# A two-layer hybrid trunk on one core: the causal mask moves from TensorE into the keys' row, and two small steps move to GpSimd and to bfloat16

## The chip, the cores and the metric

The kernel runs on one core of one Trainium2 chip: TensorE (PE, matmuls), VectorE (DVE), ScalarE (ACT), GpSimd (POOL) and SyncE (SP, which issues all the DMAs here). The metric is the time of one execution on the device in microseconds, as the median of several runs; lower is better.

## What is computed

Two layers, each a gated mixer over 1024 tokens of width 1024, with 16 heads of 64. Layer 1 is a forgetting attention: a full causal attention whose scores get a decay from a running sum `c` of log-gates. Layer 2 is a windowed attention over three dilations. Cut to what matters here:

```python
def rms_norm(x, g):
    return x * rsqrt(mean(x * x, -1) + EPS) * g

# layer 1, per head, for a block of 128 queries
s = einsum('bqhd,bkhd->bhqk', qi, k) * scale
s = s + ci[..., None] - c_k[:, :, None, :]
s = where(key_pos <= q_pos, s, -inf)
p = softmax(s)
o = einsum('bhqk,bkhd->bqhd', p, v)

# each layer
x = x + (mixer(rms_norm(x, norm_g)) * silu(gate)) @ w_out
```

## The kernel before, in words

**Projections in split float16.** Every float32 matrix is held as a high and a low float16 part. `project` (L693) multiplies 128 tokens by a block of 384 weight columns in 24 matmuls: 8 slices of the width, each as high x high, high x low and low x high. `xh` and `xl` are the two parts of the normed tokens. The weights come as blocks (`Weights`): `load` brings raw float32, `bound` (L630 on ACT, L632 on VectorE, L635) finds a bound of their size per partition in `vm2`, `scale` (L637 on) adds it over the partitions with one matmul against a matrix of ones (`spread_sums`, L602), takes a power of two from it in five small VectorE steps (L604, L592 to L594, L651 or L646), and `split` writes the two float16 parts (L658 on ACT, L659 on VectorE; one quarter by GpSimd, L661 to L663). There are 44 blocks and so 44 such sums.

**Layer 1's attention.** The work goes by pairs of heads (8), and in a pair by tiles of 128 query rows (`fox_tile`, t = 0 to 7). The keys of a tile, (t + 1) x 128 of them, are taken in pieces of 512 columns. For a piece, `scores` (L869) writes q times k into a PSUM bank `s`, two matmuls for each pair of key blocks (256 columns) or single block (128): one with `qk_t` (transposed q and k by DMA), one with `qs` (the same with the parts swapped, copied by VectorE, L849). The piece that holds the diagonal then gets a third matmul, L1114: the identity times a triangle of -1e30 (`ident_b`, `tri_b`, in bfloat16) is accumulated onto the diagonal block. VectorE's reduction (L1116) adds the keys' row `bc` (the running sum `c`, broadcast to 128 partitions by a DMA, L1082, 512 keys each, one for each head and half), negates, and keeps the smallest value. ACT takes the exponent (L912) and the high part (L915), GpSimd subtracts it to get the low part `ph` (L918), a DMA transposes both (L919), and `pv` multiplies by the values (L926 to L928).

**The start.** Eight tiles of x are normed on the way in. The factors of the first two come from columns (`column_factor`: squares on ACT, 8 matmuls with ones, L971, then steps on VectorE and ACT), those of the other six from rows (`row_factor`: squares on ACT, L952; L953, L740 to L742 and the diagonal `dg`, L956, on VectorE; two ACT steps between) and a matmul with ones (L961). `gain_xt` (GpSimd, L986) multiplies by the norm's gain, `split_xt` by the factor and writes `xh` (ACT, L993) and `xl` (VectorE and GpSimd, L994).

**What sets the order.** The program is written with a list of slots (`Flow`), 32 per head pair, one for each two of the 8 slices of a projection. Then `plan_engines` puts every engine's instructions into a fixed order: it takes each with the lengths of a small table (`Step.lasts`), gives it the latest start by which the matmuls, in the order written, would not wait, and lets the engines pick the most urgent that is ready. TensorE starts from the written order. The rotating buffers have counts by tag in `CFG`: `ga` holds the keys' rows and the tiles of x.

## Time and profile before

| | before |
|---|---|
| median of 3 runs | 1662.17 us (1659.58 to 1665.16) |
| profiled execution | 1665.39 us, span 1663.6 us |
| mean granted clock of TensorE | 0.995 |
| moved by DMA | 288.65 MB, mean 174 GB/s |

The span runs from the first to the last instruction of the program; 1.8 us of the profiled execution lie around it. In the rows that follow, a group of instructions reads: line, engine, operation, tile written <- tiles read, shapes, count, then the busy time in us and the mean length of one in ns, then the idle time of the engine ahead of them and who ended it. A row of the timeline has start and length in us. A row of waits has the waiting instruction, the one waited for, the sum in us, the count and the longest. PEld is the load of a matmul's fixed operand, which runs beside other matmuls.

### The profile page before, as it was taken

The numbers are of one execution on the slowest core, as the hardware profiler recorded it, in microseconds if no ns is written. First come the engines' busy times: TensorE is split into PE (matmuls) and PEld (weight loads), VectorE is DVE, ScalarE is ACT, GpSimd is POOL, SyncE is SP. The second block draws the span as 40 slices with busy tenths as digits, with TensorE's granted clock in tenths as the row PEclk, the third lists the DMA queues.
The fourth block names the chain that finished last, engine by engine and source line by source line (L and its number), as shares of the span: only waits on it lengthen the run. The fifth ranks groups of instructions, "written<-read, shape, count | busy, mean of one in ns | idle before, by whom it ended". The sixth has DMA issues, their size and how long they took to land.

```text
span 1663.6 us, 37721 instructions
## 1 busy us (share of the span) xinstructions
PE 1612.1 (97%) x13342; PEld 1045.5 (63%) x13342; DVE 1198.8 (72%) x3695; ACT 1063.0 (64%) x2746; POOL 893.5 (54%) x1049
## 2 busy tenths in 40 slices
PE   5999999999998899999999999999999999999999
PEld 3666677776765447666666666666666666666644
DVE  7857888878876597577676697677776777767751
ACT  6656777777776467566666686666665666666630
POOL 4303666565644242155555566676676766857430
PEclk9999999999999999999999999999999999999999
DMA  7344999999999785247776797668677577768952
GB/s 243 112 134 115 195 214 206 201 188 196 209 202 224 226 252 183 97 110 156 166 156 152 155 227 160 161 160 189 152 168 164 138 191 148 184 159 169 217 163 96
DMA packets 646477, 288.65 MB, mean 174 GB/s; under 512 B 493824, under 2 KB 610560, under 8 KB 646288
## 3 DMA queue, kind: packets, MB, share of 16 engines
q1 hardware_dynamic: 646288, 286.25, 72.7%
q8 instruction: 104, 1.70, 0.4%
q14 instruction: 85, 0.70, 0.2%
HBM read 124.35 MB, written 41.22 MB: 100 GB/s over the span
## 4 chain that ended last, share of the span: by engine, by line
PE 57%; DVE 6%; DMA 4%; issue 2%; ACT 2%; SPq 1%; POOL 1%; DVEq 0%; ACTq 0%; POOLq 0%
PE pj L693 44%; PE pj L718 7%; PE s L869 4%; DMA qk_t<-hl 2%; DVE w L659 1%; PE ob L928 1%; PE ob L926 1%; PE ob L927 1%; DVE xs L1266 1%; DMA ptt<-ph 1%; POOL ph L918 1%; DMA xn_d<-xg 1%; DMA yt<-y_d 1%; ACT w L658 1%; SPq L919 0%
## 5 line engine op out<-in xcount | busy, mean ns | idle before, releaser
L693 PE MATMUL pj<-w,xh 128*128 128x384 f16 (+2 forms) x4864 | 1174.2, 324 | 11.4 <-ACT w L658 4.8
L693 PE MATMUL pj<-w,xl 128*128 128x384 f16 (+2 forms) x2432 | 788.5, 324 | 4.2 <-DVE xl L1271 4.2
L693 PEld LDWEIGHTS <-xh 128*128 128x128 f16 x4864 | 467.3, 98 | 285.1 <-issue 10.6
L693 PEld LDWEIGHTS <-xl 128*128 128x128 f16 x2432 | 238.4, 98 | 160.1 <-issue 6.3
L918 POOL TENSOR_TENSOR ph<-p,ph 128x512 f16<-128x512 f32 (+3 forms) x176 | 174.7, 1012 | 119.5 <-issue 60.0
L1354 POOL TENSOR_TENSOR ph<-p,ph 128x768 f16<-128x768 f32 (+2 forms) x96 | 161.5, 1682 | 138.4 <-ACT ph L1353 131.0
L836 POOL TENSOR_TENSOR hl<-u,hl 128x512 f16<-128x512 f32 x128 | 150.9, 1179 | 71.5 <-ACT hl L835 59.1
L718 PE MATMUL pj<-xh,w 128*128 128x512 f16 x512 | 157.4, 379 | 7.5 <-DVE xr L1232 3.5
L869 PE MATMUL s<-qk_t 128*128 128x128 f16 (+1 forms) x1184 | 151.1, 242 | 4.7 <-DMA qk_t<-hl 4.2
L793 ACT ACTIVATE sq<-pj 128x256 f32<-128x256 f32 x256 | 96.4, 376 | 85.2 <-DVE u L788 84.4
L788 DVE TENSOR_TENSOR u<-pj,gr 128x256 f32<-128x256 f32 x256 | 107.1, 418 | 55.6 <-PE pj L693 54.2
L659 DVE SCALAR_TENSOR_TENSOR w<-raw,sws,w 128x768 f16<-128x768 f32 x96 | 135.4, 1412 | 11.3 <-ACT w L658 11.1
L912 ACT ACTIVATE p<-p,acc 128x512 f32<-128x512 f32 (+2 forms) x192 | 109.4, 607 | 45.0 <-DVE acc L1116 44.8
L718 PEld LDWEIGHTS <-w 128*128 128x128 f16 x768 | 74.0, 98 | 89.1 <-issue 8.9
L1343 ACT ACTIVATE p<-p,og 128x128 f32<-128x128 f32 (+1 forms) x256 | 104.2, 442 | 28.9 <-DVE og L1341 28.0
L926 PEld LDWEIGHTS <-ptt 128*128 128x128 f16 x1136 | 106.1, 98 | 16.5 <-DMA ptt<-ph 5.2
L927 PEld LDWEIGHTS <-ptt 128*128 128x128 f16 x1136 | 105.6, 97 | 11.4 <-issue 0.2
L630 ACT ACTIVATE jk<-raw 128x768 f16<-128x768 f32 (+2 forms) x88 | 72.1, 820 | 55.3 <-DMA raw<-in_w_dsw 36.8
L835 ACT CAST hl<-u 128x512 f16<-128x512 f32 x128 | 78.7, 615 | 45.0 <-DVE u L833 42.3
L1341 DVE CUSTOM_DVE_ANT_0 p<-s,band 128x256 f32<-128x256 f32 (+1 forms) x256 | 90.4, 373 | 23.5 <-PE s L869 23.2
L928 PEld LDWEIGHTS <-ptt 128*128 128x128 f16 x1136 | 105.7, 97 | 0.0
L820 POOL TENSOR_TENSOR ra<-u,cs 128x128 f32<-128x128 f32 x96 | 44.5, 463 | 108.5 <-DVE u L788 98.4
(213 smaller groups left out, 2985.3 us busy)
## 6 DMA issues: line engine op xcount, KB each, us to landing
raw<-in_w_dsw SPq DMA_DIRECT2D x96, 384.0 KB, 4.0
raw<-in_w_fox SPq DMA_DIRECT2D x32, 384.0 KB, 4.2
og_d<-og SPq DMA_DIRECT2D x64, 132.0 KB, 2.4
cmb<-og_d SPq DMA_DIRECT2D x64, 132.0 KB, 2.8
bc<-c_d SPq DMA_DIRECT2D x32, 256.0 KB, 4.0
gs_d<-ge SPq DMA_DIRECT2D x32, 192.0 KB, 2.0
xt<-in_xt SPq DMA_DIRECT2D x16, 256.0 KB, 5.0
gsf<-gs_d SPq DMA_DIRECT2D x64, 64.0 KB, 2.5
```

The costliest lines, as they stand in the source:

```text
L659: nc.vector.scalar_tensor_tensor(w[:, 1, :, :n], raw, self.sw, w[:, 0, :, :n], ALU.mult, ALU.subtract)
L693: nc.tensor.matmul(ps[:, :n], a[:, k, cols], w.slab(k, j), start=(k == 0 and i == 0), stop=(k == KT - 1 and i == 2))
L718: nc.tensor.matmul(ps[m], ws[h].slab(k, j)[:, m * P : (m + 1) * P], a[:, k, 512 * b : 512 * (b + 1)], start=(k == 0 and x == 0), stop=(k = ...
L788: nc.vector.tensor_mul(u[:, t % 2].rearrange("p (a b) d -> p a b d", a=2), ps[:, : 4 * HD].rearrange("p (a b d) -> p a b d", a=2, b=2), gr ...
L836: nc.gpsimd.tensor_sub(hl[:, :, :4, 1], u, hl[:, :, :4, 0])
L869: nc.tensor.matmul(s[:, c0 : c0 + cnt * P].rearrange("p (c s) -> p c s", c=cnt), q, kk[:, j : j + cnt, e], start=(h == 0), stop=(h == 1 an ...
L912: nc.scalar.activation(p, p, AF.Exp, bias=acc, scale=-1.0)
L918: (nc.gpsimd if pool_l else nc.vector).tensor_sub(ph[:, e, 1, cols], p, ph[:, e, 0, cols])
L926: nc.tensor.matmul(o[:, e, :], hi, vt[:, j, e, HD:], start=(b == 0), stop=False, skip_group_check=True)
L927: nc.tensor.matmul(o[:, e, :HD], hi, vt[:, j, e, :HD], start=False, stop=False, skip_group_check=True)
L928: nc.tensor.matmul(o[:, e, :], lo, vt[:, j, e, HD:], start=False, stop=(b == n - 1), skip_group_check=True)
L1354: nc.gpsimd.tensor_sub(ph[:, 1], st["p"], ph[:, 0])
```

## The change

Four things, in one diff. In layer 1's attention the mask matmuls go, with their two constants. The keys' row `bc` becomes 640 wide: 512 keys and ahead of them a slot of 128. For the piece with the diagonal, GpSimd writes into the slot the row's part of the diagonal block plus the triangle (one addition of 128x128 for each head and tile, 128 in all), the scores are written with the diagonal block first, and VectorE's reduction reads the slot and the keys behind it. The probabilities come out in that order, so the value matmuls take the blocks in the order `placed`. The weight bounds are copied into bfloat16 by GpSimd (`vb`) and summed against a bfloat16 matrix of ones. In `row_factor` the five VectorE steps become five GpSimd steps. And the order changes: the first weights' bounds and scale are written ahead of the second tile's factor, the planner starts its engines at 750 and its DMAs at 2400, counts early DMAs 1.35 times, and `ga` gets 8 buffers (7), `qs` 5 (6).

```diff
-    free = dict.fromkeys(ENGINES, 0.0)
+    free = dict.fromkeys(ENGINES, 750.0)
-    pool_end = lock_end = dma_end = 0.0
+    pool_end = lock_end = 0.0
+    dma_end = 2400.0
...
-            dma_end = max(dma_end, t + 500) + x.serves()
+            dma_end = max(dma_end, t + 500) + x.serves() * (1.35 if dma_end < 8000 else 1)
...
-    ident_b = const.tile([P, P], BF16, name="ident_b")
-    nc.vector.tensor_copy(ident_b, ident)
-    tri_b = const.tile([P, P], BF16, name="tri_b")
-    nc.vector.tensor_copy(tri_b, tri)
...
+    ones_b = const.tile([P, P], BF16, name="ones_b")
+    nc.gpsimd.memset(ones_b, 1.0)
...
-        nc.tensor.matmul(ws, ones.bitcast(src.dtype), src, start=True, stop=True)
+        nc.tensor.matmul(ws, by if by is not None else ones.bitcast(src.dtype), src, start=True, stop=True)
...
-            root_scale(f[:, 0:1], spread_sums(self.vm2, KT // 2), 268)
+            vb = sm.tile([P, KT // 2], BF16, name="vb", tag="vb")
+            nc.gpsimd.tensor_copy(vb, self.vm2)
+            root_scale(f[:, 0:1], spread_sums(vb, KT // 2, ones_b), 268)
...
-        nc.scalar.activation(xr, xr, AF.Square, accum_out=v[:, 1:2])
-        nc.vector.tensor_scalar(v[:, 0:1], v[:, 1:2], 1.0 / D, EPS, ALU.mult, ALU.add)
-        inv_sqrt(v[:, 3:4], v[:, 0:1], 1, v[:, 2:3])
+        m, q, a, y = (v[:, i : i + 1] for i in range(4))
+        nc.scalar.activation(xr, xr, AF.Square, accum_out=q)
+        nc.gpsimd.tensor_scalar(m, q, 1.0 / D, EPS, ALU.mult, ALU.add)
+        nc.scalar.activation(y, m, AF.Ln)
+        nc.scalar.activation(y, y, AF.Exp, scale=-0.5)
+        nc.gpsimd.tensor_mul(a, y, y)
+        nc.gpsimd.tensor_mul(a, a, m)
+        nc.gpsimd.tensor_scalar(a, a, -0.5, 1.5, ALU.mult, ALU.add)
         dg = fac[t] = sm.tile([P, P], F32, name="dg", tag="dg", bufs=2)
-        nc.vector.tensor_scalar(dg, ident, v[:, 3:4], None, ALU.mult)
+        nc.gpsimd.tensor_scalar(dg, ident, y, a, ALU.mult, ALU.mult)
...
+    for i in range(KT // 2):
+        w.bound(i)
+    w.scale()
     with book.early(nc, cfg["rush"] / 2):
         nb = column_factor(1)
         gain_xt(1)
         split_xt(1, nb)
-    for i in range(KT // 2):
-        w.bound(i)
-    w.scale()
...
-            bcs[hp, e, h] = lay([P, 512], F32, name="bc", tag="ga")
-            nc.sync.dma_start(bcs[hp, e, h], c_d[2 * hp + e, h * 512 : (h + 1) * 512].partition_broadcast(P))
+            bcs[hp, e, h] = lay([P, 5 * P], F32, name="bc", tag="ga")
+            nc.sync.dma_start(bcs[hp, e, h][:, P:], c_d[2 * hp + e, h * 512 : (h + 1) * 512].partition_broadcast(P))
...
+        a0 = pieces[-1][0] // P
+        placed = [*range(a0), t, *range(a0, t)]
...
-            runs = [(kts[j // 2], j % 2, n) for j, n in key_runs(range(a // P, b // P))]
-            scores(s, kts[t // 2], t % 2, e, runs, b < nk)
+            bc = bcs[hp, e, a // 512]
+            look = key_runs(range(a // P, b // P))
             if b == nk:
-
-                nc.tensor.matmul(s[:, t * P - a : b - a], ident_b, tri_b, start=False, stop=True, skip_group_check=True)
+                look = [[t, 1]] + key_runs(range(a // P, t))
+                nc.gpsimd.tensor_add(bc[:, :P], bc[:, b - a : b - a + P], tri)
+            scores(s, kts[t // 2], t % 2, e, [(kts[j // 2], j % 2, n) for j, n in look])
             acc = st["acc"][:, c : c + 1]
-            nc.vector.tensor_tensor_reduce(p, s[:, : b - a], bcs[hp, e, a // 512][:, : b - a], -1.0, accs[e], ALU.add, ALU.min, acc)
+            nc.vector.tensor_tensor_reduce(p, s[:, : b - a], bc[:, : b - a] if b == nk else bc[:, P:], -1.0, accs[e], ALU.add, ALU.min, acc)
```

**What stands in the engines' orders.** TensorE, in layer 1's attention, the scores of the second query tile (t = 1, two key blocks) for one head of a pair. Before, one pair of blocks and the mask:

```order
L869 LDWEIGHTS qk_t
L869 MATMUL s<-qk_t 128x256
L869 LDWEIGHTS qs
L869 MATMUL s<-qk_t,qs 128x256
L1114 LDWEIGHTS ident_b
L1114 MATMUL s<-tri_b,ident_b 128x128
```

Now the diagonal block and the other block, each alone:

```order
L870 LDWEIGHTS qk_t
L870 MATMUL s<-qk_t 128x128
L870 LDWEIGHTS qs
L870 MATMUL s<-qk_t,qs 128x128
L870 LDWEIGHTS qk_t
L870 MATMUL s<-qk_t 128x128
L870 LDWEIGHTS qs
L870 MATMUL s<-qk_t,qs 128x128
```

The mask's matmul is gone, and where the tile's number is odd two matmuls of 256 columns stand as four of 128.

POOL, in the same stage, from the first tile of a head pair (`ph` of 128x2x128) to the fifth (128x512 and 128x128, the third in time). Before, subtractions and one low part of q and k:

```order
L918 TENSOR_TENSOR ph_4461<-p_4449,ph_4461 128x2x128
L918 TENSOR_TENSOR ph_4535<-p_4523,ph_4535 128x2x256
L836 TENSOR_TENSOR hl_4504<-u_4406,hl_4504 128x8x64
L918 TENSOR_TENSOR ph_4597<-p_4584,ph_4597 128x512
L918 TENSOR_TENSOR ph_4597<-p_4591,ph_4597 128x128
```

Now (`bc_4403` and `bc_4466` are the rows of the second half of the keys for the two heads, `bc_3801` and `bc_4061` those of the first half, `vb` the next weights' bounds):

```order
L919 TENSOR_TENSOR ph_4523<-p_4511,ph_4523 128x2x128
L1122 TENSOR_TENSOR bc_4403<-bc_4403,band_93 128x128
L640 CAST vb_4803<-vm2_4580 128x4
L1122 TENSOR_TENSOR bc_4466<-bc_4466,band_93 128x128
L1122 TENSOR_TENSOR bc_3801<-bc_3801,band_93 128x128
L1122 TENSOR_TENSOR bc_4061<-bc_4061,band_93 128x128
L919 TENSOR_TENSOR ph_4601<-p_4585,ph_4601 128x2x256
L837 TENSOR_TENSOR hl_4566<-u_4468,hl_4566 128x8x64
L1122 TENSOR_TENSOR bc_4403<-bc_4403,band_93 128x128
L1122 TENSOR_TENSOR bc_4466<-bc_4466,band_93 128x128
L919 TENSOR_TENSOR ph_4663<-p_4650,ph_4663 128x512
L919 TENSOR_TENSOR ph_4663<-p_4657,ph_4663 128x128
```

Six additions and the copy have come between the subtractions: the first two of the second half's rows are for the fifth tile, the two of the first half's for the third, the last two for the sixth.

VectorE, in the first 20 us, around the reduction of the first weights' sum (`v<-ws`; `cf` and `nb` are steps of a column factor, `xt` a tile of x). Before:

```order
L975 TENSOR_SCALAR cf<-nb 128x128
L991 TENSOR_TENSOR xt_128<-xt_128,nb 128x512
L604 TENSOR_REDUCE v_240<-ws 128x1
L953 TENSOR_SCALAR nv<-nv 128x1
L632 TENSOR_REDUCE vm<-raw 128x1
L994 TENSOR_TENSOR xl<-xt_126,xh 128x4x128
L592 TENSOR_SCALAR v_240<-v_240 128x1
L632 TENSOR_REDUCE vm<-raw 128x1
L593 TENSOR_SCALAR v_240<-v_240 128x1
L979 SCALAR_TENSOR_TENSOR nb<-nb,cf 128x128
L594 TENSOR_SCALAR ws_f<-v_240 128x1
L980 SCALAR_TENSOR_TENSOR nb<-nb,dg 128x128
```

Now:

```order
L981 TENSOR_SCALAR cf<-nb 128x128
L603 TENSOR_REDUCE v_212<-ws 128x1
L591 TENSOR_SCALAR v_212<-v_212 128x1
L592 TENSOR_SCALAR v_212<-v_212 128x1
L593 TENSOR_SCALAR ws_f<-v_212 128x1
L652 TENSOR_SCALAR ws_f<-ws_f,sx 128x1
L985 SCALAR_TENSOR_TENSOR nb<-nb,cf 128x128
L653 RECIPROCAL ws_f<-ws_f 128x1
L986 SCALAR_TENSOR_TENSOR nb<-nb,dg 128x128
L997 TENSOR_TENSOR xt_124<-xt_124,nb 128x512
L631 TENSOR_REDUCE vm<-raw 128x1
L997 TENSOR_TENSOR xt_126<-xt_126,nb 128x512
```

The weights' chain, spread between other steps before and behind the first tile, stands in one piece ahead of the first tile's multiply.

More of the change, by code (lines that the diff above doesn't have):

```diff
@@ L594, in root_scale, with spread_sums @@
         nc.vector.tensor_single_scalar(dst.bitcast(I32), e, 0x7F800000, ALU.bitwise_and)
-    def spread_sums(src, n):
+    def spread_sums(src, n, by=None):
         if under.get("ps") is not None:
@@ L862, in key_runs, with scores @@
         return runs
-    def scores(s, qk, i, e, keys, more):
+    def scores(s, qk, i, e, keys):
         c0 = 0
@@ L873, in scores @@
                     start=(h == 0),
-                    stop=(h == 1 and not more),
+                    stop=(h == 1),
                     skip_group_check=True,
@@ L1128, in score @@
                 for i in range(2):
-                    ptl[i] = [(pt[:, i, 0, j], pt[:, i, 1, j], j) for j in range(t + 1)]
+                    ptl[i] = [(pt[:, i, 0, k], pt[:, i, 1, k], j) for k, j in enumerate(placed)]
             else:
@@ L1133, in score @@
                 pt = p_transpose(1, nk, exps, splits)
-                ptl[e] = [(pt[:, 0, 0, j], pt[:, 0, 1, j], j) for j in range(t + 1)]
+                ptl[e] = [(pt[:, 0, 0, k], pt[:, 0, 1, k], j) for k, j in enumerate(placed)]
         def values(e):
@@ L1332, in score @@
                 for e in range(2):
-                    scores(ss[i][:, 2 * e * P :], qks[1], i, e, keys, False)
+                    scores(ss[i][:, 2 * e * P :], qks[1], i, e, keys)
             for i in range(2):
@@ L1500, in trunk @@
     layer["cm"].__exit__(None, None, None)
-CFG = dict(out={(False, 0): (), (True, 0): ((18, 20, 22, 24), (0, 0, 1, 1), 3, (4, 6, 8, 10)), (True, 1): ((18, 20, 22, 24), (14, 15, 17, 18), 24, (33, 35, 37, 39))}, take=(((33, 34, 37, 40), 42), ((62, 63, 66, 69), 71)), rush=2000, gate=(((6, 7, 8, 9), (0, 0, 1, 1), 4, (5, 6, 7, 9)), ((44, 45, 46, 47), (26, 28, 30, 32), 36, (38, 40, 42, 44)), ()), bc=((1, 0, 26), (1, 1, 28), (0, 0, 38), (0, 1, 46)), wpool=3, rbufs=8, most=(0, 2), lcm=7, ps=0, pv=100, ph_=100, ph=1, wbufs=8, pl=3, um=3, lpf=8, lsd=((16, 16), (16, 14), (14, 11)), ty2=((0, 4), (1, 5)), hb=2, ub=2, qb=1, nb=3, fox=(((0, 0, 2, 2), (2, 4)), ((0, 0), (4, 4))), due=(29, 33, 39, 45, 35, 41, 49, 57), l1=dict(ga=7, ptt=4, ph=3, p=4, qk_t=6, qs=6, vt=3, gsl=3), l2=dict(ga=4, cmb=4, gsd=4, ptt=3, ph=3, p=2, qk_t=3, og=3, vt=3, gsl=3, par=1), wload=(18, 20, 22, 24), wbound=(0, 1, 3, 4), wscale=8, wsplit=(10, 16, 22, 12))
+CFG = dict(out={(False, 0): (), (True, 0): ((18, 20, 22, 24), (0, 0, 1, 1), 3, (4, 6, 8, 10)), (True, 1): ((18, 20, 22, 24), (14, 15, 17, 18), 24, (33, 35, 37, 39))}, take=(((33, 34, 37, 40), 42), ((62, 63, 66, 69), 71)), rush=2000, gate=(((6, 7, 8, 9), (0, 0, 1, 1), 4, (5, 6, 7, 9)), ((44, 45, 46, 47), (26, 28, 30, 32), 36, (38, 40, 42, 44)), ()), bc=((1, 0, 26), (1, 1, 28), (0, 0, 38), (0, 1, 46)), wpool=3, rbufs=8, most=(0, 2), lcm=7, ps=0, pv=100, ph_=100, ph=1, wbufs=8, pl=3, um=3, lpf=8, lsd=((16, 16), (16, 14), (14, 11)), ty2=((0, 4), (1, 5)), hb=2, ub=2, qb=1, nb=3, fox=(((0, 0, 2, 2), (2, 4)), ((0, 0), (4, 4))), due=(29, 33, 39, 45, 35, 41, 49, 57), l1=dict(ga=8, ptt=4, ph=3, p=4, qk_t=6, qs=5, vt=3, gsl=3), l2=dict(ga=4, cmb=4, gsd=4, ptt=3, ph=3, p=2, qk_t=3, og=3, vt=3, gsl=3, par=1), wload=(18, 20, 22, 24), wbound=(0, 1, 3, 4), wscale=8, wsplit=(10, 16, 22, 12))
 def host_layout(inputs):
```

## The prediction

> **What bounds the kernel now.** I read the page first, for the shares of the engines:
>
> ```profile
> span 1663.6 us, 37721 instructions
> PE 1612.1 (97%) x13342; PEld 1045.5 (63%) x13342; DVE 1198.8 (72%) x3695; ACT 1063.0 (64%) x2746; POOL 893.5 (54%) x1049
> ```
>
> TensorE is busy for 97% of the span; it leaves 51.5 us over. A share of the whole span says nothing on a stage, so the second view is the busy time by stage: the stretch up to 60 us is the start, 130 to 450 most of the eight head pairs of layer 1's attention, 450 to 560 its tail. The columns are PE, weight loads, DVE, ACT and POOL busy, then the granted clock, the DMA share and GB/s.
>
> ```profile
> 0.00:20.00 20.00, 6.86 (x36) 6.50 (x37) 9.75 (x35) 11.51 (x27) 7.41 (x15) 1.00 0.82 289
> 20.00:40.00 20.00, 16.42 (x90) 9.57 (x90) 19.16 (x39) 14.19 (x30) 11.67 (x11) 0.83 0.58 189
> 130.00:300.00 170.00, 169.11 (x1711) 118.46 (x1709) 138.22 (x439) 124.00 (x317) 97.32 (x93) 1.00 0.86 187
> 300.00:450.00 150.00, 148.05 (x1579) 105.78 (x1577) 125.07 (x406) 112.62 (x282) 93.20 (x91) 1.00 0.95 201
> 450.00:560.00 110.00, 98.21 (x946) 63.89 (x945) 71.58 (x210) 73.97 (x157) 52.89 (x50) 0.98 0.94 210
> ```
>
> In the attention TensorE is idle for 2.8 of 320 us, while DVE is 82% and POOL 60% busy: matmuls set the time there, and a matmul that is taken out is time won as long as nobody else becomes late. In the first 40 us TensorE is idle for 16.7 us: there the chain that feeds it sets the time. The third view, TensorE's waits in 130 to 450 us, holds only two lines:
>
> ```profile
> PE s L869 <- DVE qs L849: 1.3, 2, 0.7
> PE o L926 <- DMA ptt<-ph: 1.2, 1, 1.2
> ```
>
> The same view up to 60 us names the start's (us in total, times, longest):
>
> ```profile
> PE pj L693 <- ACT w L658: 4.8, 1, 4.8
> PE pj L693 <- DVE w L659: 4.2, 3, 1.8
> PE nb L961 <- DVE nv L953: 0.6, 1, 0.6
> ```
>
> **The mask matmuls.** The groups by form give their count, and the timeline of TensorE at one of them its price in the stream (start, length):
>
> ```profile
> L1114 PE MATMUL s<-tri_b,ident_b 128*128 128x128 bf16 x128 | 27.7, 220 | 0.0
> ```
> ```profile
> 252.74 0.27 PE L869 MATMUL s<-qk_t,qs 128*128 128x256 f16 x1
> 252.85 0.22 PE L869 MATMUL s<-qk_t 128*128 128x128 f16 x1
> 252.91 0.22 PE L869 MATMUL s<-qk_t,qs 128*128 128x128 f16 x1
> 252.96 0.22 PE L1114 MATMUL s<-tri_b,ident_b 128*128 128x128 bf16 x1
> 253.02 0.27 PE L869 MATMUL s<-qk_t 128*128 128x256 f16 x1
> ```
>
> The 220 ns of a matmul overlap with its neighbours; what it costs is the distance to the next start: 0.055 us for 128 columns (252.91, 252.96, 253.02), 0.11 for 256. 128 masks x 0.056 = 7.2 us leave the stream. Against that, the diagonal block now stands alone and first, so a row tile with an odd number loses its last pair of key blocks: 8 head pairs x 4 odd tiles x 2 heads = 64 times, two matmuls of 256 columns become four of 128, 4 x 0.056 - 2 x 0.109 = 0.006 us, together 0.4 us. Net 6.8 us.
>
> **What GpSimd gets for it.** 128 additions of 128x128. The trace has the same shape, two operands from SBUF, in another stage, and beside it the work that POOL has in the attention (130 to 530 us):
>
> ```profile
> L820 POOL TENSOR_TENSOR ra<-u,cs x96: 446/453/1266, 704.3 to 1566.2; 128x128 f32<-128x128 f32 x96
> ```
> ```profile
> L918 POOL TENSOR_TENSOR ph<-p,ph 128x512 f16<-128x512 f32 x102 | 119.0, 1176 | 110.8 <-issue 56.2 <-ACT ph L915 25.7 <-ACT rs_y L827 15.8
> ```
>
> 128 x 0.45 = 58 us over about 370 us of attention take POOL from 60% to some 76%: off the path as long as each addition ends before VectorE wants the row. In the order, the additions for a tile stand four to ten POOL instructions ahead of its own subtraction, and VectorE wants the row some three ahead of that; an instruction there takes about 1 us, so I cost the place at nothing. What is queued behind an addition that waits for its row's DMA is the subtraction of another tile, and its transpose and value matmuls behind that; the issue to landing of a row is 4.0 us at the median, and a row is asked for at least 7 of a head pair's 32 slots ahead of its first use, 7 x 47 / 32 = 10 us. The second cost lies on VectorE, whose operations slow down when POOL works:
>
> ```profile
> L849 DVE TENSOR_SCALAR qs<-qk_t x64: 286/346/1274, 140.0 to 511.9; 64x256 int32<-64x256 int32 x64
> L659 DVE SCALAR_TENSOR_TENSOR w<-raw,sws,w x96: 999/1182/2894, 97.3 to 1512.4; 128x768 f16<-128x768 f32 x96
> ```
>
> The lowest and the largest length differ by one long POOL operation. The Trainium skill states the rule behind that ("SBUF — State Buffer", section "SBUF: two separate sides"): VectorE and GpSimd share a pair of ports, an instruction holds it to its end, and an instruction of the other that needs it waits. It speaks against this change, since every addition is one more holder; the trace agrees as far as the spread of these two rows goes. From the rows alone: some 11 such VectorE operations per head pair (8 qs, 3 weight splits) could each be held for up to 0.45 us, 5 us of the 8 us that VectorE has idle in a head pair (18% of 47 us). At POOL's added share (16%) it is nearer to 1 us. I take +1.2 us for the whole stage (bounds 0 and 7, the latter the whole gain).
>
> **The sums of the weight bounds.** 44 matmuls of 128x4 go from float32 to bfloat16. Two that follow each other, and the stream around the second:
>
> ```profile
> 300.86 0.30 PE L602 MATMUL pj<-vm,ones 128*128 128x4 f32 x1
> ...
> 336.21 0.19 ACT L635 ACTIVATE vm<-vm 128x2 fp32r<-128x2 f32 x1
> ...
> 347.12 0.49 PE L693 MATMUL pj<-w,xh 128*128 128x384 f16 x2
> 347.45 0.33 PE L693 MATMUL pj<-w,xl 128*128 128x384 f16 x1
> 347.48 0.30 PE L602 MATMUL pj<-vm,ones 128*128 128x4 f32 x1
> 347.64 0.50 PE L693 MATMUL pj<-w,xh 128*128 128x384 f16 x2
> 347.98 0.33 PE L693 MATMUL pj<-w,xl 128*128 128x384 f16 x1
> ```
>
> From 347.45 to 347.98 stand three projection matmuls, 3 x 0.163 = 0.49 us of 0.53: the sum costs 0.04 us. (From 300.86 to 347.48 is a head pair, 47 us, the figure used above.) A bfloat16 one can save between nothing and all of it, 0 to 1.8 us over 44; I take 0.3. The copy into bfloat16 lies on POOL between the bound and the sum. This bound had its last piece at 336.4, 11 us ahead of the matmul, which covers it; where a new layer's weights follow at once that cover is gone, and two or three times up to 0.5 us show: +0.3.
>
> **The start.** The rows that carry it:
>
> ```profile
> 10.03 0.83 ACT L630 ACTIVATE jk<-raw 128x768 f16<-128x768 f32 x1
> 10.97 1.26 ACT L969 ACTIVATE xsq<-xt 128x512 f32<-128x512 f32 x2
> 14.55 1.04 ACT L952 ACTIVATE xrow<-xrow 128x1024 f32<-128x1024 f32 x1
> 15.17 0.25 PE L602 MATMUL ws<-vm,ones 128*128 128x4 f32 x1
> 16.79 0.16 DVE L604 TENSOR_REDUCE v<-ws 128x1 f32<-128x4 f32 x1
> 19.28 3.41 ACT L658 ACTIVATE w<-raw,ws_f 128x768 f16<-128x768 f32 x4
> 20.26 0.32 PE L693 MATMUL pj<-w,xh 128*128 128x384 f16 x1 [4.84 <-ACT w L658]
> 25.36 0.52 PE L693 MATMUL pj<-w,xl 128*128 128x384 f16 x1
> 26.15 1.00 DVE L659 SCALAR_TENSOR_TENSOR w<-raw,ws_f,w 128x768 f16<-128x768 f32 x1
> ```
>
> Today the first weights' bounds are ready at about 11, but the sum stands on TensorE behind the second tile's column sums (15.17), its reduction on VectorE behind that tile's work (16.79), and the first half of the weights is written from 19.28. The change puts the sum ahead of the second tile. Then: copy on POOL until 11.3, sum and five small VectorE steps until 12.5. ACT is next in the way: its order holds two steps of the first factor (0.6), the row's squares (1.2), the third step (0.3) and the second tile's squares (1.26) ahead of the split, 10.9 + 3.4 = 14.3. First weights at 15.2, xh of the first tile at 15.9: TensorE starts at about 16 in place of 20.26. VectorE writes the four low halves in between other steps, the last at about 22.6 in place of 27.15 (it waits for ACT's third step of tile 1 at about 21). So the first tile's 24 matmuls are done near 24. The second tile needs its factor behind that, then a multiply of 0.7 and a cast of 0.6: about 25.5. Before, 9 of the 24 had started by 25.4. Ahead by 15 x 0.163 = 2.4 us. Behind it comes the factor of the third tile, now on POOL behind a step that waits for ACT; and 1.8 us of waiting for the second weight block (the longest of the three above) that may fall away, since VectorE is rid of five small steps per tile. I take 3.0 us for the start, bounds 0 (all of it waits again for the third tile's factor) and 5.4 (2.4 + 1.8 + two waits of 0.6).
>
> **The sum.** -7.2 + 0.4 - 0.3 + 1.2 + 0.3 - 3.0 = -8.6 us. The profiled execution took 1665.39 us (1.8 around its span) and lies 3.2 above the median of 1662.17; taken off the median the forecast is 1653.6. The rest of layer 1's tail and layer 2 stand in the same order as before, so nothing is booked there.
>
> **The rivals.** *The attention gives it back.* The 6.8 us return as waits of TensorE on qs, on transposes or on DMA (its share is 0.95 in 300 to 450, and in the tail, 450 to 560, TensorE is idle for 11.8 us). Against it: 2.5 us of waits in 320, and none on the rows. Then only the start is won: 1662.2 - 3.0 = 1659.2, no measurable change. *Slower: the additions come late.* If they wait on POOL behind subtractions that wait themselves, VectorE stands before its reduction with everything behind it. VectorE has 8 us idle in a head pair and 16 additions: up to 0.5 us each is free, and there it decides. Ten of 16 late by one subtraction (1.18 us) would be 11.8 - 8 = 3.8 us per head pair, 30 in all: 1684. For it speak POOL's waits before the subtractions (the row of L918: 110.8 us idle), against it that the additions stand ahead of their tile by several of these. *Full clock from the start.* TensorE waited 4.8 us in one piece ahead of 20.26, and from there the clock fell to 0.83 over 20 us, 3.4 us lost. After the change, by the working above, no piece reaches 3 us. If the clock then never falls, up to 3.4 us more: 1650.2. The Trainium skill has this as a rule ("TensorE: Matmul & The Clock Gate", section "What's actually happening"): an idle window of about 3.4 us brings half clock, and as long a busy one ends it. The trace agrees in that the fall follows its longest wait; that the wait shrinks is only my estimate. *The start wins nothing*, as a wait on the third tile's factor takes its place: 1662.2 - 5.6 = 1656.6.
>
> **How the numbers follow.** Three runs of before lie 5.6 us apart; 0.3% (5.0 us) is about what can be told from no change, so faster means below 1657.2. Forecast 0.52, of it 0.48 below that line; given back 0.20, all within; full clock 0.10, faster; start without gain 0.10, half of it on each side; late additions 0.08, slower. Faster 0.63, same 0.29, slower 0.08. The range goes down to the full clock with the start's upper bound (1650.2 - 2.4, less another 0.8 for the sums' own bound) 1647, and up over the case of a given-back gain by what a median can be off, to 1662; outside lie the late additions and a little more.
>
> **What would show it.** Right: no line for the mask, 256-column score matmuls fewer by 128 and 128-column ones more by 256; 128 additions of about 0.45 us; in 130 to 450 us still under 5 us of TensorE waits; first projection matmul near 16; an attention shorter by 6 us. Wrong: VectorE's reductions waiting on the additions, qs longer by a third with TensorE behind it, or the first 60 us without more matmuls than before.

## The result and the profile after

| | before | after |
|---|---|---|
| median of 6 runs | 1662.30 us (1659.58 to 1665.16) | 1652.52 us (1652.01 to 1656.83) |
| ratio to before | | 0.9936 [0.9922, 0.9949] |
| profiled execution | 1665.39 us, span 1663.6 | 1656.83 us, span 1654.8 |

The kernel is faster by 9.8 us at the median. The profiled executions differ by 8.6 us, the same as the sum of the forecast; each is the slowest of its six. In the tables below, places in the stream are marked by the start of a projection matmul that both programs have: the 701st (in the first head pair, 137.84 us before) ends the start, the 2113th (600.87 us) is the first of layer 2.

| in the profiled execution | before | after | difference |
|---|---|---|---|
| first projection matmul | 20.26 | 16.38 | -3.9 |
| end of the start (701st) | 137.84 | 133.43 | -4.4 |
| from there to layer 2 (2113th) | 463.03 | 458.44 | -4.6 |
| layer 2 and its end | | | +0.2 |

First the stages of after, with the same columns as before: PE, weight loads, DVE, ACT and POOL busy, then the granted clock, the DMA share and GB/s.

```profile
0.00:20.00 20.00, 11.39 (x49) 8.95 (x50) 11.66 (x32) 14.02 (x30) 10.18 (x20) 1.00 0.92 335
20.00:40.00 20.00, 16.29 (x92) 9.56 (x91) 17.82 (x31) 15.10 (x37) 19.46 (x29) 0.91 0.53 185
130.00:300.00 170.00, 165.86 (x1716) 115.98 (x1714) 135.29 (x443) 124.62 (x316) 126.27 (x158) 1.00 0.92 192
300.00:450.00 150.00, 148.96 (x1638) 106.75 (x1637) 125.31 (x411) 116.68 (x290) 118.85 (x147) 1.00 1.01 206
```

In the first 40 us TensorE is busy for 4.4 us more (27.7 against 23.3). In 130 to 450 POOL went from 60% to 77%, and TensorE's idle time from 2.8 to 5.2 us. Its waits in that stretch name where (5.1 us in all; the forecast had set under 5 as a sign of being right):

```profile
PE o L927 <- DMA ptt<-ph: 4.1, 4, 1.5
PE s L870 <- DVE acc L1125: 1.0, 1, 1.0
```

The waits for `qs` are gone; those for transposed probabilities went from 1.2 to 4.1 us. The additions, by form, with the idle time of GpSimd ahead of them and who ended it:

```profile
L1122 POOL TENSOR_TENSOR bc<-bc,band 128x128 f32<-128x128 f32 x128 | 65.6, 524 | 28.3 <-DMA bc<-c_d 13.3 <-DVE acc L1125 13.1 <-ACT w L659 1.1
```

An addition is 0.52 us at the mean (0.46 at the median), but GpSimd also stands still for 28.3 us in front of them: 13.3 for the row's DMA, 13.1 for the reduction that still reads the slot for the tile before. From 130 to 450 us it is 15.2 us. One such wait can be followed to TensorE. On GpSimd's timeline the second row waits, with two subtractions behind it; on SP's the row was asked for at 216.92, and the transpose of the first of those subtractions, issued at 218.56, is held for 5.56 us; on TensorE's the value matmul then waits:

```profile
218.40 1.23 POOL L1122 TENSOR_TENSOR bc<-bc,band 128x128 f32<-128x128 f32 x1
221.88 0.45 POOL L1122 TENSOR_TENSOR bc<-bc,band 128x128 f32<-128x128 f32 x1 [2.25 <-DMA bc<-c_d]
222.30 2.08 POOL L919 TENSOR_TENSOR ph<-p,ph 128x512 f16<-128x512 f32 x2
```
```profile
216.92 0.57 SPq L1088 DMA_DIRECT2D bc<-c_d  x1
218.56 5.56 SPq L920 DMA_TRANSPOSE ptt<-ph  x1
```
```profile
226.15 0.20 PE L927 MATMUL o<-vt,ptt 128*128 128x65 f16 x1 [1.47 <-DMA ptt<-ph]
```

This row is asked for 5 us ahead of its first reader, not 10: the planner put the addition far ahead of VectorE's use. In 8 of the 32 rows the addition waits for the DMA like this. So there were two theories for what the attention gives back: waits at the head of GpSimd's queue (A), or DMAs that are full and bring transposes late whoever adds (B).

The start, on the timeline:

```profile
10.20 0.19 POOL L640 CAST vb<-vm 128x4 bf16<-128x4 f32 x1 [0.20 <-ACT jk L629]
10.43 0.16 PE L601 MATMUL ws<-vb,ones_b 128*128 128x4 bf16 x1 [0.46 <-POOL vb L640]
13.17 0.92 ACT L659 ACTIVATE w<-raw,ws_f 128x768 f16<-128x768 f32 x1
16.38 0.85 PE L694 MATMUL pj<-w,xh 128*128 128x384 f16 x2
20.58 1.01 DVE L660 SCALAR_TENSOR_TENSOR w<-raw,ws_f,w 128x768 f16<-128x768 f32 x1
23.73 0.50 PE L694 MATMUL pj<-w,xh 128*128 128x384 f16 x2
```

The walk of the forecast holds within a microsecond or two: copy at 10.2 (forecast until 11.3), weights from 13.2, first matmul at 16.38 (16), last low half done at 21.6 (22.6), second tile from 23.7 (25.5).

### The profile page after: what moved, and what is told of

The parts are those of the page before. It is cut to its first block, busy times and chain, and to the rows that moved or that the text cites. A ratio compares the mean times of both kernels' runs of the same rounds, so it can differ in the third digit from the quotient of the medians.

```text
span 1654.8 us, 37873 instructions
## 1 busy us (share of the span) xinstructions
PE 1605.9 (97%) x13342; PEld 1037.5 (63%) x13342; DVE 1192.6 (72%) x3663; ACT 1063.5 (64%) x2746; POOL 963.9 (58%) x1252
## 4 chain that ended last, share of the span: by engine, by line
PE 74%; DVE 10%; DMA 6%; ACT 4%; issue 3%; POOL 2%; SPq 0%; DVEq 0%; POOLq 0%; ACTq 0%
PE pj L694 56%; PE pj L719 7%; PE s L870 6%; DMA qk_t<-hl 3%; DVE w L660 2%; DVE p L1125 1%; PE ob L929 1%; PE ob L927 1%; PE ob L928 1%; DMA ptt<-ph 1%; ACT w L659 1%; PE o L929 1%; PE o L927 1%; PE o L928 1%; DVE xl L1280 1%
## 5 line engine op out<-in xcount | busy, mean ns | idle before, releaser
L1363 POOL TENSOR_TENSOR ph<-p,ph 128x768 f16<-128x768 f32 (+2 forms) x96 | 157.7, 1642 | 137.6 <-ACT ph L1362 130.1
L660 DVE SCALAR_TENSOR_TENSOR w<-raw,sws,w 128x768 f16<-128x768 f32 x96 | 146.6, 1528 | 11.0 <-ACT w L659 10.7
L1350 DVE CUSTOM_DVE_ANT_0 p<-s,band 128x256 f32<-128x256 f32 (+1 forms) x256 | 90.7, 373 | 22.8 <-PE s L870 22.6
```

The lines of the kernel that those rows point to most:

```text
L660: nc.vector.scalar_tensor_tensor(w[:, 1, :, :n], raw, self.sw, w[:, 0, :, :n], ALU.mult, ALU.subtract)
L1363: nc.gpsimd.tensor_sub(ph[:, 1], st["p"], ph[:, 0])
```

## The experiments

All ratios are to the kernel before, run on the same chip. 0.001 is 1.7 us. The kernel before stood in every set of runs, the changed kernel in the first set alone, so a difference between two runs is one of ratios. The three columns at the right are differences to before in the profiled execution, in us; one execution differs from another of the same kernel by several us, so they tell where, and the ratios how much.

| run | ratio [interval] | start | attention and its tail | layer 2 |
|---|---|---|---|---|
| changed kernel | 0.9936 [0.9922, 0.9949] | -4.4 | -4.6 | +0.2 |
| e1, zero matmuls added | 1.0000 [0.9989, 1.0012] | -4.9 | +3.1 | +0.9 |
| e2, masks by matmul | 0.9973 [0.9962, 0.9984] | -4.8 | -2.9 | -0.3 |
| e10, new mask alone | 0.9995 [0.998, 1.0009] | -0.5 | +0.4 | +4.3 |
| e3, a quarter of the additions | 0.9947 [0.9928, 0.9966] | -4.3 | -4.6 | +3.5 |
| e4, each addition twice | 1.0047 [1.0033, 1.0061] | -4.4 | +13.9 | +1.3 |
| e11, rows early | 1.0039 [1.0024, 1.0054] | -4.0 | +9.4 | +0.8 |
| e12, new mask alone, rows early | 1.0061 [1.0037, 1.0086] | +0.7 | +6.0 | +0.9 |
| e13, additions planned later | 1.0022 [1.0009, 1.0035] | -4.2 | +6.3 | -0.5 |
| e14, additions on VectorE | 1.0010 [0.9998, 1.0022] | -4.0 | +1.9 | +2.5 |
| e8, sums in float32 | 0.9956 [0.994, 0.9972] | -6.8 | -0.8 | +2.4 |
| e5, first scale late | 0.9954 [0.9938, 0.9971] | -4.0 | -3.7 | +1.4 |
| e6, row factors on VectorE | 0.9970 [0.9955, 0.9985] | -1.5 | -5.9 | +5.5 |

**e1: is a mask matmul worth 0.056 us?** The changed kernel with 128 matmuls of the old size put back, on zeros. (The scores of the diagonal block, the only thing that they write, do not survive them: the result lacks these, and the kernel stands for its time alone.)

```diff
...
-            scores(s, kts[t // 2], t % 2, e, [...])
+            scores(s, kts[t // 2], t % 2, e, [...], b == nk)
+            if b == nk:
+                nc.tensor.matmul(s[:, :P], ones_b, zero_b, start=False, stop=True, skip_group_check=True)
```

> The changed kernel, with 128 matmuls of 128x128 bfloat16 put back where the mask's stood; they add zeros, so the additions on GpSimd still do the masking. Theory of the stream (a matmul taken out of the attention is time won): 128 x 0.056 = 7.2 us come back, 1659.5 to 1660. Rival, that the attention was gained by the order and the buffers and not by the matmuls: within 1.5 us of the changed kernel, 1651 to 1654. Between the two: part of the stream's time lay in waits anyway.

The whole gain goes: 0.0064 +- 0.0018 or 10.6 us over the changed kernel, and 7.7 us in the stage itself (+3.1 against -4.6). The price of 7.2 is near the stage's figure and just under the lower end of the other (7.6 to 13.6 us).

**e2: everything but the mask.** The changed kernel with the old mask scheme (two constants, `bc` 512 wide, blocks in their old order).

```diff
-                look = [[t, 1]] + key_runs(range(a // P, t))
-                nc.gpsimd.tensor_add(bc[:, :P], bc[:, b - a : b - a + P], tri)
...
+                nc.tensor.matmul(s[:, t * P - a : b - a], ident_b, tri_b, start=False, stop=True, skip_group_check=True)
```

> The changed kernel with the mask as before (matmul of the identity and the triangle, keys' row of 512 without a slot, key blocks in their old order), everything else changed. Theory of the stream: 6.8 us come back less the 1 us or so that the additions cost, 1657 to 1659. Theory that the additions cost nothing: 1659. Rival, order and buffers: 1652 to 1654.

The rest alone gives 4.5 us at the median. So in this company the mask is worth 0.0037 +- 0.0017, or 6.2 us, where the forecast had 5.6 (7.2 - 0.4 - 1.2). The profiled executions show less of it: the start of e2 has -4.8, but its attention -2.9 too, which leaves 1.7 for the mask. (That execution of e2 is the second fastest of its twelve, the changed kernel's the slowest of its six.) What the mask took out of the stream shows in TensorE's busy time between the 701st and the 2113th projection matmul, before, in e2 and after:

```profile
137.84:600.87 463.03, 448.40 (x4370) 302.03 (x4368) 362.17 (x1105) 330.75 (x778) 255.43 (x239) 1.00 0.92 207
133.08:593.22 460.14, 448.56 (x4371) 300.90 (x4368) 356.87 (x1106) 332.51 (x779) 258.79 (x250) 1.00 0.93 208
133.43:591.87 458.44, 441.86 (x4370) 295.32 (x4369) 359.01 (x1106) 330.81 (x779) 314.50 (x376) 1.00 0.96 209
```

With the mask by matmul TensorE is busy for 448.4 and 448.6 us, without it for 441.9: 6.5 and 6.7 us less, where the forecast had 6.8. (The clock stood at half for 3.4 us of the stage in each of the three.) Its idle time is 14.6, 11.6 and 16.6 us. From 130 to 450 us e2 idles for 2.9 us, as before; so the 2.3 us more in the changed kernel come with the new scheme.

**e10: the mask without the rest.** The kernel before with the slot, the additions, the new order of blocks and the buffer counts.

```diff
-CFG = dict(... l1=dict(ga=7, ..., qs=6, ...) ...)
+CFG = dict(... l1=dict(ga=8, ..., qs=5, ...) ...)
...
+                look = [[t, 1]] + key_runs(range(a // P, t))
+                nc.gpsimd.tensor_add(bc[:, :P], bc[:, b - a : b - a + P], tri)
```

> The kernel before with the new mask alone (slot, additions, key order, and the buffer counts 8 and 5), start and sums as before. Theory of the stream: 1662.3 - 5.5 = 1657, with the attention shorter by 4 to 6 us and the first 130 us as before. Rival, that the start carries nearly all: 1661 to 1662.

No measurable gain, 0.8 us; the rival of this run came out. The same edit is worth 6.2 us in one company and 0.8 in another. In its profile the matmuls did leave the stream: between the same two projection matmuls TensorE is busy for 445.6 us (448.4 before), although the clock stood at half for 10.2 us of the stage there (3.4 before), and it idles for 17.8 us (14.6 before). That execution is 5.8 us slower than the median of its kernel. Why the gain is lost in this company isn't settled: the other edits also move the order that the planner gives, and e11 and e13 below show what another order of the same work can do.

**e3: fewer additions.** Only the tiles t = 0 and 4 get an addition (32 of 128; the other tiles read the slot as that one left it, with the triangle but with another block's part of the row).

```diff
+                if t % 4 == 0:
                     nc.gpsimd.tensor_add(bc[:, :P], bc[:, b - a : b - a + P], tri)
```

> The changed kernel with the addition written only for the first tile of each keys' row, 32 in place of 128; the other tiles read the slot as that one left it, so their mask and keys' term in the diagonal block are left wrong. If the additions lie beside other work: within 1.5 us, 1651 to 1654. If they hold up VectorE or the subtractions (the shared ports, the queue), three quarters of what they cost goes: 1647 to 1650, with fewer waits of value matmuls on transposes.

As the changed kernel (0.0011 +- 0.0023 above it). 42 us less of GpSimd's work from 130 to 450 us buys nothing that shows, so between 32 and 128 the number is no cost that can be told. What remains is the first addition on each row, which waits for its DMA (6.6 us in 8 waits): that spoke for theory A. But TensorE's waits for transposed probabilities were to fall with the additions and didn't: 7.0 us in seven, 4.1 in the changed kernel.

**e11: the rows earlier.** One line, and the same work.

```diff
-CFG = dict(... bc=((1, 0, 26), (1, 1, 28), (0, 0, 38), (0, 1, 46)), ...)
+CFG = dict(... bc=((1, 0, 16), (1, 1, 18), (0, 0, 28), (0, 1, 36)), ...)
```

> The changed kernel with one line other: the keys' rows are asked for 10 slots of 32 (some 15 us) earlier. Theory A (rows too late for their new first reader): in the changed kernel an addition that waits for its row's DMA stands at the head of GpSimd's queue and holds subtractions, transposes and value matmuls behind it (6.1 us in 5 waits from 130 to 450 us, and 4.9 us of TensorE waits for transposed probabilities over the run). With the rows early the additions' waits for a DMA fall below 2 us, TensorE's waits for transposes fall by 2 to 4 us, and the time is 1649 to 1651 where the changed kernel has 1652.5 (ratio to before 0.992). Rival B (the transposes are late because the DMAs are full, share 0.92 to 1.0): the additions stop waiting but TensorE waits for transposes as before, 4 to 6 us; ratio 0.9935, no change to the changed kernel. Rival C (order): the rows now come in between transposes that are urgent, and the time rises by 1 to 4 us.

The sign is rival C's, the size none of the three: slower than the changed kernel by 0.0103, 17 us. TensorE's waits from 130 to 450 us, then those of GpSimd's additions:

```profile
PE o L927 <- DMA ptt<-ph: 6.5, 7, 1.8
PE s L870 <- DVE acc L1125: 2.4, 3, 1.0
PE pj L694 <- DVE u L834: 2.1, 1, 2.1
PE s L870 <- DMA qk_t<-hl: 1.6, 2, 0.9
```
```profile
POOL bc L1122 <- DVE acc L1125: 13.4, 13, 2.7
POOL bc L1122 <- DMA bc<-c_d: 7.0, 6, 2.2
```

An addition that is ready earlier in the plan is also put earlier in GpSimd's order. It waits no less for the row (7.0 against 6.1 us), and longer for the reduction that still reads the slot (13.4 against 7.4); with the smaller ones the waits grew from 15.2 to 28.0 us.

**e12: the mask alone, rows early.** The same line in e10.

> The kernel before with the new mask alone (slot, additions, buffer counts 8 and 5) and the keys' rows asked for 10 slots earlier. With the rows at their old slots this part alone gave a ratio of 0.9995. Theory A (late rows ate the mask's gain): the gain of 6.8 us shows up, at least 4 of it: ratio 0.996 to 0.9975. Rival B (DMA saturation or another order ate it): 0.999 to 1.001 again. Rival C (the gain is lost behind the attention, in layer 2, by another order of the planner): the attention ends 3 to 6 us earlier in the trace than before and the total does not.

11 us slower than e10. Asking earlier does not bring the mask's gain back. It is no clean test of late rows, though: the additions moved forward with the rows, and from 130 to 450 us they wait for them longer than in e10 (17.8 us against 9.7).

**e4: each addition twice.**

```diff
                 nc.gpsimd.tensor_add(bc[:, :P], bc[:, b - a : b - a + P], tri)
+                nc.gpsimd.tensor_add(bc[:, :P], bc[:, b - a : b - a + P], tri)
```

> The changed kernel with each of the 128 additions issued twice (the second writes the same values again): 58 us more of GpSimd's work over 370 us, its share in the attention from 77% to about 92%. With a quarter of the additions (32) the ratio was 0.9947, with 128 it is 0.9936: no price for their number so far. Theory A (the number costs nothing while GpSimd has room, only waits at the head of its queue cost): within 3 us of the changed kernel, ratio 0.993 to 0.9955. Rival B (shared port: each addition costs VectorE or TensorE a little): +1.2 us for 128 as the forecast had it, ratio 0.9945. Rival C (GpSimd becomes the bound of the attention, subtractions late at every tile): +5 to +30 us, ratio 0.997 to 1.012.

Rival C: +18 us over the changed kernel, at 85% busy of GpSimd in 130 to 450 us against 77%. That GpSimd has no room left at 85% is the plain reading, but not shown: the order is another one too, and e13 below loses 14 us at 74%.

**e13: the additions later.** In the planner, an addition counts as ready 1 us later.

```diff
-                ready[j] = max(ready[j], end[k] + tail + SIGNAL[q] + margin[q])
+                ready[j] = max(ready[j], end[k] + tail + SIGNAL[q] + margin[q] + (1000 if q == "Pool" and steps[j].outs[0].name.startswith("bc") else 0))
```

> The changed kernel with the planner told that an addition can start 1 us later behind what it waits for, so that on GpSimd it is put later, behind subtractions; the work is the same. Asking for the rows 10 slots earlier moved the additions forward in GpSimd's order: their waits at the queue's head went from 15 to 28 us between 130 and 450 us, and the time up by 17 us. Theory A (waits at the head of GpSimd's queue): the additions' waits fall below 10 us, and the time is 1648 to 1653 (ratio 0.991 to 0.994). Rival B (any other order than the one found for these lengths is worse, since the order was fitted to them): ratio 0.997 to 1.005 with the waits for the additions no longer than in the changed kernel. Rival C: the additions now come too late for VectorE's reductions, which then wait on them in the trace: over 5 us of such waits, ratio above 0.998.

Slower than the changed kernel by 14 us, though the additions' waits fell from 15.2 to 11.6 us in 130 to 450 (theory A had asked for under 10):

```profile
PE o L927 <- DMA ptt<-ph: 5.8, 4, 2.4
PE s L870 <- DVE acc L1125: 3.4, 3, 1.7
PE pj L694 <- DVE u L834: 1.4, 1, 1.4
```
```profile
POOL bc L1122 <- DVE acc L1125: 10.5, 8, 2.5
POOL bc L1122 <- DMA bc<-c_d: 1.1, 1, 1.1
```

TensorE's waits went up to 10.6 us all the same. So theory A falls as the one cause: the length of the waits at the head of GpSimd's queue doesn't order the results (11.6 us in e13, 15.2 after, 28.0 in e11). Rival B of this run, another order is a worse one, is what came out; what in the order does it stays open.

**e14: nothing of it on GpSimd.**

```diff
-                nc.gpsimd.tensor_add(bc[:, :P], bc[:, b - a : b - a + P], tri)
+                nc.vector.tensor_add(bc[:, :P], bc[:, b - a : b - a + P], tri)
```

> The changed kernel with the 128 additions on VectorE, whose reductions stand behind one another anyway; GpSimd has none. Theory A (what eats the mask's gain is GpSimd's queue: an addition that waits at its head for a row or for the reduction that reads its slot, 15 us in 5 + 12 + 1 + 1 waits from 130 to 450 us, holds subtractions, transposes and value matmuls): TensorE's waits for transposed probabilities fall from 4.1 us to under 2 in that stretch, and the time is 1649 to 1652 (ratio to before 0.991 to 0.993), as long as VectorE, 81% busy there, has room for 128 x 0.25 us = 32 us more (10%). Rival B (transposes are late because the DMAs are full, whoever adds): the waits for transposes stay, ratio 0.9936 as the changed kernel. Rival C (VectorE becomes late): waits of TensorE on VectorE's qs and reductions, 5 to 15 us, ratio 0.997 to 1.003.

Rival C. TensorE's waits, and the two stages:

```profile
PE s L870 <- DVE qs L850: 6.3, 4, 2.0
PE o L927 <- DMA ptt<-ph: 2.9, 5, 1.1
```
```profile
130.00:300.00 170.00, 164.18 (x1693) 114.13 (x1692) 155.22 (x485) 122.39 (x310) 96.65 (x96) 1.00 0.91 186
300.00:450.00 150.00, 145.51 (x1591) 103.31 (x1590) 142.56 (x460) 114.64 (x285) 93.37 (x94) 1.00 0.98 206
```

VectorE goes from 81% to 93%, and its `qs` comes late for 6.3 us. The waits for transposes fall only from 4.1 to 2.9 with no addition in GpSimd's queue at all. They don't follow the additions in the other profiles either: 1.2 before and 2.6 in e2, both without additions, 7.0 in e3 with a quarter of them.

**e8: the sums in float32**, without the copy `vb`.

```diff
-            vb = sm.tile([P, KT // 2], BF16, name="vb", tag="vb")
-            nc.gpsimd.tensor_copy(vb, self.vm2)
-            root_scale(f[:, 0:1], spread_sums(vb, KT // 2, ones_b), 268)
+            root_scale(f[:, 0:1], spread_sums(self.vm2, KT // 2), 268)
```

> The changed kernel with the 44 sums of the weight bounds in float32 again, without the copies to bfloat16 on GpSimd. The forecast had -0.3 us for the bfloat16 matmuls (bounds 0 to -1.8) and +0.3 for exposed copies: together nothing, ratio 0.9936 and the first projection matmul within 0.3 us of 16.4. Rival: a float32 matmul of 4 columns stops the stream for more than the 0.04 us read from one place (weight load of 128x128 float32 in four passes); then 44 x 0.1 to 0.3 us come back, 4 to 13 us, ratio 0.996 to 1.001.

0.0020 +- 0.0021 above the changed kernel, no difference that can be told. (Its profile has a start shorter by 2.4 us and an attention longer by 3.8; one profile can't tell whether these are the edit's.) The rival's weight load took 0.19 us in float32 before (at 347.45) where bfloat16's takes 0.10 (at 296.60), beside running matmuls. In the stream of the changed kernel one sum stands like this:

```profile
296.60 0.33 PE L694 MATMUL pj<-w,xl 128*128 128x384 f16 x1
296.76 0.17 PE L601 MATMUL pj<-vb,ones_b 128*128 128x4 bf16 x1
296.79 0.48 PE L694 MATMUL pj<-w,xh 128*128 128x384 f16 x2
297.12 0.32 PE L694 MATMUL pj<-w,xl 128*128 128x384 f16 x1
```

Three projection matmuls and the sum take 0.52 us where before they took 0.53: 0.01 x 44 = 0.4 us saved, an estimate at the resolution of the rows.

**e5 and e6: which edit made the start.** e5 writes the first weights' bounds and scale behind the second tile's factor again; e6 gives the row factors' five steps back to VectorE.

```diff
-    for i in range(KT // 2):
-        w.bound(i)
-    w.scale()
     with book.early(nc, cfg["rush"] / 2):
...
+    for i in range(KT // 2):
+        w.bound(i)
+    w.scale()
```
```diff
-        nc.gpsimd.tensor_scalar(m, q, 1.0 / D, EPS, ALU.mult, ALU.add)
...
+        nc.vector.tensor_scalar(v[:, 0:1], v[:, 1:2], 1.0 / D, EPS, ALU.mult, ALU.add)
+        inv_sqrt(v[:, 3:4], v[:, 0:1], 1, v[:, 2:3])
...
+        nc.vector.tensor_scalar(dg, ident, v[:, 3:4], None, ALU.mult)
```

> The changed kernel with the bounds and the scale of the first weights written again behind the second tile's factor. The start (to the 700th projection matmul, ahead of the attention) ends 4.4 us earlier in the changed kernel than in the one before; the forecast had 3.0, all from this move. If so: first projection matmul at 19 to 20.5 where the changed kernel has 16.4, and the start's gain falls to 0 to 1.5 us; ratio 0.995 to 0.997. Rival (the row factors on GpSimd and the planner's constants bring it): the first matmul goes back but the start keeps over 2.5 us of its gain.

> The changed kernel with the five small steps of the row factors on VectorE again. The forecast had up to 1.8 us for VectorE's relief in its bound, not in its value, and 0 as the other end if the third tile's factor is late on GpSimd. Theory A: the start's gain falls from 4.4 to 2.6 to 4 us; ratio 0.994 to 0.995. Rival (GpSimd's factors come later than VectorE's would, three waits of 0.3 to 0.8 us on the factor's diagonal in the changed kernel): the start gains 0.5 to 1.5 us more, ratio 0.9925 to 0.9935.

| start of a projection matmul | before | changed | e5 | e6 |
|---|---|---|---|---|
| 1st | 20.26 | 16.38 | 19.95 | 17.35 |
| 24th (last of the first tile) | 29.09 | 22.30 | 28.35 | 27.91 |
| 701st | 137.84 | 133.43 | 133.82 | 136.36 |

Without the early scale the first matmul comes late again, and the start still wins 4.0 us. With it and without the moved factors the first matmul comes early and 1.5 us are left. (The seven other runs that keep the moved factors, the early scale and the copy have -4.0 to -4.9; e8, without the copy, -6.8.) TensorE's waits up to 60 us in e5, then in e6:

```profile
PE nb L967 <- POOL dg L962: 1.2, 2, 0.8
PE pj L694 <- DVE w L660: 0.8, 1, 0.8
```
```profile
PE pj L694 <- DVE w L660: 5.6, 4, 2.8
PE nb L962 <- DVE nv L954: 0.7, 1, 0.7
```

In e6 TensorE waits for the weights' low halves on VectorE, 5.6 us in four waits (4.2 in three before); with the row factors off VectorE, 0.8 in e5.

## Why the prediction was right, point by point

**The total** came out by 1.1 us (1653.6 forecast, 1652.5 measured), and both of its large terms have the right sign and about the right size. That the sum fits this closely is luck: the attention gained 1.0 us less than forecast (4.6 for 7.2 - 0.4 - 1.2 = 5.6), the start 1.4 more (4.4 for 3.0). Two steps under them were wrong.

**The mask matmuls, -7.2 + 0.4.** Right: TensorE's busy time in the stage fell by 6.5 us for 6.8 (6.7 against e2), putting as many back costs 7.7 us there (e1), and no mask line is left in the trace; there are 128 score matmuls fewer of 256 columns and 256 more of 128, as forecast.

**The additions' place, "I cost the place at nothing".** This step failed. It rested on rows asked for 10 us ahead and on additions standing well ahead of VectorE's use. The row followed above came 5 us ahead of its first reader, 8 of 32 made their addition wait, and an addition that stands early is one that can wait. In this very order the price is small: TensorE's idle time in 130 to 450 rose by 2.4 us where the forecast took 1.2, and 6.8 - 2.4 = 4.4 us is near what the stage shows (-4.6). Other orders of the same instructions cost 14 to 17 us more (e13, e11). What was missing in the forecast is that the result hangs on the order: in e13, where the plan lets an addition start 1 us later, and in e11 waits for transposes and reductions grow together and others for `u` or `qk_t` come up (TensorE's idle time in 130 to 450: 5.2 us after, 10.8 in e13, 13.9 in e11).

**The price on VectorE, +1.2 with bounds of 0 and 7.** The four rows are the weights' low halves from 130 to 450 us (lowest, median, largest length in ns): before and in e14, with no addition on GpSimd, in the changed kernel, and in e13.

```profile
L659 DVE SCALAR_TENSOR_TENSOR w<-raw,sws,w x20: 999/1146/1904, 131.1 to 418.3; 128x768 f16<-128x768 f32 x20
L660 DVE SCALAR_TENSOR_TENSOR w<-raw,sws,w x18: 1000/1013/1815, 178.0 to 423.5; 128x768 f16<-128x768 f32 x18
L660 DVE SCALAR_TENSOR_TENSOR w<-raw,sws,w x18: 998/1170/1820, 160.4 to 405.3; 128x768 f16<-128x768 f32 x18
L660 DVE SCALAR_TENSOR_TENSOR w<-raw,sws,w x18: 1004/1620/2119, 168.1 to 419.8; 128x768 f16<-128x768 f32 x18
```

The same operation takes from 1.0 to 2.1 us. The change itself hardly moved its median (1146 to 1170), and the number of additions doesn't set it: e13 has as many as the changed kernel and 1620, e4 twice as many and 1318. The rule in the Trainium skill ("SBUF — State Buffer", section "SBUF: two separate sides"), one holder of the shared ports at a time, would give such spreads; no run here takes the ports apart from the order. So the 1.2 us themselves are not shown. In the changed kernel none of it reached TensorE by way of `qs`: no wait on it is left in this stretch.

**The sums, -0.3 and +0.3.** Right in that they make no difference that can be told (e8), and 0.4 us by the stream.

**The start, -3.0.** It is -4.4, within the bound of 5.4; the wrong step is the one that says why. The forecast credited the early scale (first matmul near 16, which came true) and kept VectorE's relief from five small steps per tile for the bound. The runs turn this round: with the moved factors and without the early scale 4.0 us are left (e5), with the early scale and without the moved factors 1.5 (e6), and the mask alone, with neither, has 0.5 (e10). So in the finished kernel the moved factors carry 2.9 us of the start and the early scale 0.4; the two don't add up, and the planner's constants, which e5 and e6 both keep, were not tried apart. The rival that the third tile's factor takes all of it back didn't come; its waits are 1.0 us in three.

**Full clock from the start** came half true. The granted clock before, and after:

```profile
20.00:22.00 2.00, 0.32 (x1) 0.10 (x1) 2.00 (x3) 2.00 (x4) 2.00 (x3) 0.68 0.79 167
26.00:28.00 2.00, 2.00 (x9) 1.10 (x8) 2.00 (x6) 0.21 (x1) 0.00 (x0) 0.62 0.00 0
```
```profile
24.00:26.00 2.00, 1.10 (x7) 0.51 (x6) 2.00 (x4) 0.57 (x2) 2.00 (x3) 0.90 0.02 8
26.00:28.00 2.00, 2.00 (x9) 1.27 (x8) 2.00 (x3) 1.95 (x4) 2.00 (x4) 0.50 0.67 229
28.00:30.00 2.00, 2.00 (x11) 1.11 (x10) 1.93 (x8) 1.92 (x6) 2.00 (x2) 0.75 0.12 41
```

Of the first pair of rows, the clock before was low from some 20.7 to 27.5 us, a loss of at most 3.4 (0.17 x 20 us by the stage). After, it still fell, later and for half as long, from some 25.6 to 29.0: at most 1.8 (0.09 x 20). It was no full clock at first either: two matmuls of 384 columns take 0.85 us at 16.38 and 0.50 at 23.73 (the rows of the start above), though the view counts the first 20 us as 1.00. Nor is the difference a part of the start's gain that can be booked. In e14, with the start's edits as they are, the clock is full from 20 to 40 us,

```profile
20.00:40.00 20.00, 16.18 (x101) 9.49 (x99) 18.89 (x35) 16.54 (x40) 19.48 (x27) 1.00 0.63 215
```

and the start has -4.0; e4, at 1.00 as well, has -4.4, and e2, at 0.83 and 0.91 in the first two stretches of 20 us, -4.8. Only e8, at 1.00 and without the copy `vb`, is better, with -6.8. The rival's 3.4 us more didn't come with the full clock in e14 and e4.

**The attention gives it back** (the rival of 1659.2) is what happens in e10 and e14 (+0.4 and +1.9 in the stage), and with the additions doubled or placed otherwise more than that. **Late additions** is not the mechanism of any of these: VectorE's reductions wait for an addition 2.5 us in e11 and 2.6 in e4, from 130 to 450.

**What stays open.** Why the order of the changed kernel loses 2.4 us and those of e11 and e13 some 11 to 14 more isn't settled beyond TensorE's waits: each of them has several causes at once, and no run takes them apart. VectorE, with the same instructions, is busy between the 701st and the 2113th projection matmul for 359 us after, 365 in e11 and 371 in e13, so its operations are longer where the kernel is slower; whether that is a cause or comes along isn't shown, and e5, at 362, loses nothing in the attention that can be told. No run moves the order of the kernel before, so it isn't known whether that one is as sensitive. Nor was it tried what the planner's constants (750, 2400, 1.35) bring by themselves, or whether a better order exists for the new mask. Layer 2, for which nothing was booked, came out between -0.5 and +5.5 us over these profiles. Part of it are waits for the transposes of q and k; from 640 us on, in the profile before, after, and in e3:

```profile
PE s L869 <- DMA qk_t<-hl: 4.2, 4, 1.5
```
```profile
PE s L870 <- DMA qk_t<-hl: 5.1, 6, 1.8
```
```profile
PE s L870 <- DMA qk_t<-hl: 7.9, 7, 1.9
```

What sets their length in one execution isn't known, which is why the stages are compared here beside the medians. None of the twelve beats the changed kernel.

## What to carry to other kernels

An edit that takes matmuls out of a stage where TensorE sets the time is worth their distance in the stream, provided that the engine which gets the work has room and its order fits; compute the first from the timeline, and take the second as a question of several per cent of that stage (14 to 17 us of 458 here), which no share of busy time told beforehand here. When work is put into the queue of an engine that others depend on, ask of each piece when its last input comes (the DMA, and the release of what it overwrites), not only when its reader wants it: a place ahead of that is a wait for everything behind it, as in the one followed here. Whether a later place is better has to be measured: in e13 it was worse. To find which of several edits made a gain, undo each alone: the one with the visible mark (the first matmul 3.9 us earlier) was not the one with most of the start's gain.

## What was not expected of the hardware

The clock fell in the changed kernel although no wait between its first projection matmul and the fall at 25.6 us is longer than 0.9 us. What precedes it is a thin stretch: TensorE is busy for 1.10 of the 2 us from 24 to 26, between waits of 0.5 and 0.9 us. The Trainium skill ("TensorE: Matmul & The Clock Gate", section "What's actually happening") asks for an idle window of about 3.4 us. No run here shows how little work in such a window counts as idle, but a wait of that length isn't needed.

VectorE's addition of 128x128 in float32 takes 0.29 us at the median (e14), GpSimd's 0.46, so on VectorE the same work costs a third less; e14 still lost, with VectorE 93% busy.
